# Chain states on ScalarE, attention outputs beside chain outputs, a gate product in rounded parts, and narrower reads in a hybrid attention/RWKV layer

## The chip, the cores and the metric

The kernel runs on one core of a Trainium2 chip. The metric is the device time of one execution in microseconds; the median of several runs is compared. PE is TensorE's matmul, PEld its weight load, DVE is VectorE, ACT ScalarE, POOL GpSimd, SP the engine that issues most DMAs.

## The reference

One layer over 16 meta tokens and 512 tokens of width 1024. A projection of 5632 columns feeds windowed attention with sinks, an RWKV-7 recurrence and two gates; both results are gated, added, projected and normalized; a squared-ReLU MLP of width 4096 and a last normalization follow. The first 16 rows are dropped.

```python
proj = h @ w_in[l]
q, k, v, zr, gate_att, gate_rwkv = jnp.split(proj, [c0, c1, c2, c3, c4], axis=-1)
att = lax.map(lambda qkv: swa_one(qkv[0], qkv[1], qkv[2], rel_bias, sinks_l), (q, k, v))
rw = rwkv7_time_mix(zr, ...)
merged = jax.nn.sigmoid(gate_att) * att + jax.nn.sigmoid(gate_rwkv) * rw
h = layer_norm(ALPHA * h + merged @ w_out[l], ...)
ff = jnp.square(jax.nn.relu(h @ w_ff1[l])) @ w_ff2[l]
h = layer_norm(ALPHA * h + ff, ...)
...
# in rwkv7_time_mix, with z shifted by one token: z + (prev - z) * mu
g = jax.nn.sigmoid(gl) @ g2
def step(S, inp):
    r_t, w_t, k_t, v_t, kk_t, a_t = inp
    sa = jnp.einsum('bhij,bhj->bhi', S, -kk_t)
    S = S * w_t[:, :, None, :] + sa[..., None] * (kk_t * a_t)[:, :, None, :] + v_t[..., None] * k_t[:, :, None, :]
    return S, jnp.einsum('bhij,bhj->bhi', S, r_t)
```

The outputs y of the meta tokens are not used by anything; their effect on the state S is.

## The kernel before

**Large products.** Every weight is split into a rounded part and its rest, both of a type that TensorE multiplies at its fast rate: ScalarE casts (`split`, line 256), VectorE subtracts (line 259). A product is then three matmuls per block of 128 rows: high by high, high by low, low by high (`three`, lines 340 to 342). A *dense unit* makes 128 columns of the input projection: 8 blocks of 3 matmuls, over all 528 tokens in two halves of 264 columns (`ALLT`, and `RSP` for the r units), or over the 512 tokens in one piece (`XT_`). A unit is a generator: one step is one block, three matmuls, and it tells the planner its length, 3 * (0.014 + n / 2400), line 371. When a span is done ScalarE and VectorE take it out of PSUM and mix in the token before (`shifted`, lines 415 to 426).

**Stages.** The 16 heads are worked off in 8 pairs. In stage s the dense units of several pairs run: the gates of pair s-1, k, r and v of pair s+1, and the query of pair s. Between their steps stand the small matmuls of three pairs: the inner scores and block inverse of pair s (`scan`), the solution of pair s-1 (`solve`), and the attention of pairs s-1 and s-2 (`attend`, `attend_out`, `join`).

**The order on PE is written by hand.** Each item has a time; `weave` sorts them and puts an item between the dense steps as soon as the sum of the steps' lengths reaches its time. PE keeps to this order strictly: an item that isn't ready holds up everything behind it. On the other engines a list scheduler sets the order at build time, by priority (`ahead` raises it: 600 for the chain, 400 for evictions, 200 for folds) and by the times that it assumes; at run time each engine's queue is worked in that order.

**The chain.** The recurrence runs over 8 blocks of 64 tokens. `rwkv_fold` (two halves, lines 876 and 881) adds the parts of the transition matrices, on VectorE, into `AX`. `rwkv_chain(j, c)` is one matmul (line 936) from state `Z[c]` into the PSUM bank `ch`; `follow` scales the result into `Z[c + 1]`, one head by VectorE (line 892), the other by ScalarE (line 894). So a link is matmul, two scalings, next matmul. `rwkv_start` uses `follow` too. `rwkv_outputs` (line 953) reads all states; `rwkv_norm` turns the result and line 977 writes it into `z`, of which there is one buffer.

**Attention.** `attention_scores` (two halves) puts products into two PSUM banks of the pool `pat`, which has two; VectorE masks and adds the bias (1108, 1109). After the second half VectorE takes the maxima, and ScalarE makes eight exponentials (1130) and eight scalings (1136). One stage later `attention_turn` transposes the probabilities, ScalarE and VectorE take them out (1151, 1152), and `attention_out` multiplies them with the values into a bank of `pat`, held from its first half to the end of its second; VectorE then multiplies with the gate in place, in `ga` (1172). `merge` adds this to `z` and stores it.

**The rest that is touched.** `gate_rank` makes `sg`, the sigmoid of the gate's low rank, once; `gate_out` multiplies it per pair with `gw`, in full fp32 (line 1088). `rwkv_bonus` makes a sum over a head with two matmuls of 512 columns (595, 596) in a bank of the pool `pg`, which the folds use too. `first_up` loads the first MLP weights into buffers that are free by then.

Of the kernel before, what the change touches and what calls it, by code (L numbers as in the profile page):

```python
# [11 lines left out]
F32 = mybir.dt.float32  # L12
F32R = mybir.dt.float32r
I32 = mybir.dt.int32
AF = mybir.ActivationFunctionType
ALU = mybir.AluOpType
# [4 lines left out]
P = 128  # L21
D = 1024
KT = D // P
SEQ = 512
# [6 lines left out]
NCH = SEQ // C  # L31
PAIRS = HEADS // 2
# [41 lines left out]

CONSTS = {}
PRI = {'load': 100, 'dense': 400, 'scores': 300, 'chain': 600, 'turn': 200, 'up': 300, 'fold': 200, 'start': 200}
RSP = ((0, 264), (264, 264))
HOLD = 4
SBB = 2
WB = (3, 3, 2)  # L80
# [1 line left out]
PS = (2, 2, 1, 1, 2)  # L82
AHEAD = 2
NBUF = {'AX': 2, 'BK': 1, 'NT': 2, 'GR': 2}
ABUF = {'q': 2, 'ga': 1, 'gg': 1, 'pa': 1, 'z': 1, 'bv': 1}


def _constants():
# [42 lines left out]
def hybrid_layer_kernel(ctx: ExitStack, tc: tile.TileContext, I: dict, out: bass.AP):  # L131
    nc = tc.nc
    dve, act, pool, pe = nc.vector, nc.scalar, nc.gpsimd, nc.tensor
# [4 lines left out]
    pg = pps.enter_context(tc.tile_pool(name="pg", bufs=PS[1], space=PSUM))  # L138
    ppr = ctx.enter_context(ExitStack())
    pch = ppr.enter_context(tc.tile_pool(name="pch", bufs=1, space=PSUM, side="right"))  # L140
    pat = ppr.enter_context(tc.tile_pool(name="pat", bufs=PS[4], space=PSUM, side="right"))
# [22 lines left out]
    lz = ctx.enter_context(tc.tile_pool(name="lz", bufs=1))  # L164
# [174 lines left out]
    def three(ps, whi, wlo, xhi, xlo, first=True, last=True):  # L339
        pe.matmul(ps, whi, xhi, start=first, stop=False)  # L340
        pe.matmul(ps, whi, xlo, start=False, stop=False)  # L341
        pe.matmul(ps, wlo, xhi, start=False, stop=last)  # L342
# [61 lines left out]
    at = p2.enter_context(tc.tile_pool(name="at", bufs=1))  # L404
    pew = ctx.enter_context(ExitStack())
    ew = pew.enter_context(tc.tile_pool(name="ew", bufs=1))
# [22 lines left out]


    zz = lz.tile([P, T], F32, name="zz", tag="zz")
    sg = lz.tile([P, SEQ], F32, name="sg", tag="sg")

    rest = CONST.shape[1]
    nc.sync.dma_start(con[:, w0:rest], I["consts"][:, w0:rest])
# [10 lines left out]
        act.copy(zz[HD:P], zl[HD:P])  # L446

    def gate_rank(zg):
        act.activation(sg, zg[:, NMETA:], AF.Tanh, scale=0.5)
        dve.tensor_scalar(sg, sg, 0.5, 0.5, op0=ALU.mult, op1=ALU.add)  # L450

    def B64(ap, n):
        return ap.unsqueeze(len(ap.shape)).to_broadcast(list(ap.shape) + [n])
# [2 lines left out]
    ER = [slice(0, 64), slice(64, 128)]  # L456
# [133 lines left out]
    def rwkv_bonus(j):  # L590
        S = SS[j]
        rkh, rkl = S["rk"]
        S["bv"] = dr.tile([P, SEQ], F32, name=f"bv{j}")
        bp = pg.tile([P, 512], F32, name="bp", tag="g")
        pe.matmul(bp, bones, rkh, start=True, stop=False)
        pe.matmul(bp, bones, rkl, start=False, stop=True)
        bv = ew.tile([P, SEQ], F32, name="bv", tag="rk")
        dve.tensor_tensor(bv, bp, S["v"][:, NMETA:], op=ALU.mult)
        nc.sync.dma_start(S["bv"], bv)
# [286 lines left out]
    def follow(S, c, src, last):  # L886

        Z, PC = S["Z"], S["PC"]
        for e in range(2):
            dst, scale = Z[c][ER[e], e, :], PC[ER[e], last : last + 1]  # L890
            if e == 0:
                dve.tensor_scalar(dst, src[e][ER[e]], scale, None, op0=ALU.mult)  # L892
            else:
                act.activation(dst, src[e][ER[e]], AF.Copy, scale=scale)  # L894

    def rwkv_start(j, n):

# [97 lines left out]
    A = {}  # L995
# [76 lines left out]

    def aside_gate_rwkv(j):

        gw = at.tile([P, P], F32, name="gw", tag="gw", bufs=2)
        nc.sync.dma_start(gw, I["gate_w2"][j])

        def evict(ps, t0, n):
            t = gate_tile("gg", "r", j)
            act.activation(t, ps, AF.Tanh, scale=0.5)  # L1080
            A["gg", j] = t

        A["gw", j] = gw
        yield from dense(COL_GRW + j * P, XT_, evict)

    def gate_out(j):
        gp = pat.tile([P, 512], F32, name="gp", tag="a")
        pe.matmul(gp, A["gw", j], sg, start=True, stop=True)
        t = A["gg", j]
        dve.scalar_tensor_tensor(t, t, 1.0, gp, op0=ALU.add, op1=ALU.mult)  # L1090

# [151 lines left out]
    for n, pools in enumerate((((dn, "dn"), (pat, "a")), ((pg, "g"), (pch, None)))):  # L1243
        for b in range(4):
            pool_, tag = pools[b // 2]
# [20 lines left out]
    def first_up():  # L1266

        A["w1"] = load_pieces("w_ff1", 0, [
            [lz.tile([P, SEQ], F32R, name="w1", tag=t, bufs=ABUF.get(t, 1)) for t in tags]
            for tags in (("zz", "sg"), ("kk", "q"))  # L1270
        ])

    def out_unit(n, blocks, asks):
# [62 lines left out]
    j = PAIRS - 1  # L1336
# [18 lines left out]
    F = partial  # L1355

    def scan(j):

        need = (f"k{j}", f"r{j}", f"v{j}")
        return [  # L1360
            (0.0, need, F(rwkv_scores, j, 0)),
            (3.2, (), F(rwkv_meta, j)),
            (3.2, (), F(rwkv_scores, j, 1)),
            (3.2, (), F(rwkv_inverse, j)),
            (5.6, (), F(rwkv_bonus, j)),
            (12.55, (), F(rwkv_turn_scores, j)),
            (18.6, (), F(rwkv_turn_keys, j)),
            (16.0, (), F(rwkv_inverse_place, j)),
            (23.2, (), F(rwkv_turn_values, j)),
        ]  # L1370

    def solve(j):

        last = j == PAIRS - 1
        return [
            (0.0, (), F(rwkv_blocks, j, 0)),
            (0.0, (), F(rwkv_start, j, 0)),
            (1.4, (), F(rwkv_blocks, j, 1)),
            (1.4, (), F(rwkv_start, j, 1)),
            (3.2, (), F(rwkv_blocks, j, 2)),  # L1380
            (3.2, (), F(rwkv_start, j, 2)),
            (4.6, (), F(rwkv_blocks, j, 3)),
            (6.4, (), F(rwkv_turn_inverse, j)),
            (8.4, (), F(rwkv_fold, j, 0)),
            (10.6, (), F(rwkv_fold, j, 1)),
        ] + [(10.4 + 1.25 * c, (), F(rwkv_chain, j, c)) for c in range(NCH - 1)] + [
            (18.61 + 0.6 * last, (), F(rwkv_outputs, j)),
            (24.6 - 1.4 * last, (), F(rwkv_norm, j)),
        ]
# [11 lines left out]
    def attend(j, t0, dt=3.6):  # L1401
        return [
            (t0, (f"q{j}",), F(attention_scores, j, 0)), (t0 + dt, (), F(attention_scores, j, 1)),
        ]

    def attend_out(j, t0, t1, t2, t3):
        return [
            (t0, (), F(attention_turn, j, 0)),
            (t1, (), F(attention_out, j, 0)),
            (t2, (), F(attention_turn, j, 1)),  # L1410
            (t3, (f"ga{j}",), F(attention_out, j, 1)),
        ]

    def join(j, t0, t1, t2):
        return [
            (t0, (f"gr{j}",), F(gate_out, j)), (t1, (), F(merge_rwkv, j)), (t2, (), F(merge, j)),
        ]

    with tc.manual_schedule(engines={mybir.EngineType.PE}):
        for s in range(-1, PAIRS + 1):  # L1420
            if s <= PAIRS:
                units[:] = [u for u in all_units[: marks[s + 1]] if u[0] not in finished]
            items = []
            if s > 0:
                items += solve(s - 1)
            if 0 <= s < PAIRS:
                items += scan(s)
            if s == -1:
                items += [
                    (0.0, (), F(rwkv_begin, 0)),  # L1430
                    (9.0, ("wa",), F(rwkv_lora, 0, 0)),
                    (10.4, (), F(rwkv_lora, 0, 1)),
                    (20.0, ("k0",), F(rwkv_sums, 0)),
                    (24.0, ("k0",), F(rwkv_begin, 1)),
                ]
            if 0 <= s < PAIRS - 1:
                items += project_in(s + 1)
            if s == 0:
                items += [(18.0, ("av",), F(aside_heads, 0))]
            if s == 4:  # L1440
                items += [(26.0, (), F(aside_heads, 1))]
            if s in (1, 5):
                items += [(2.4, (), turn_heads)]
            if 0 < s < PAIRS - 1:
                items += attend(s - 1, 4.6, 1.8) + join(s - 1, 13.5, 25.4, 0)[:2]
            if 1 < s < PAIRS:

                items += attend_out(s - 2, 7.6, 8.4, 9.4, 10.6) + join(s - 2, 0, 0, 11.6)[2:]
            if s == PAIRS - 1:
                items += [(14.0, (), merged_before)]  # L1450
                items += attend(s - 1, 4.6, 1.8) + attend_out(s - 1, 15.6, 16.6, 16.6, 18.0)
                items += join(s - 1, 15.0, 26.5, 26.5)
                items += attend(s, 11.6, 2.2)
                items += [(27.2, (), F(load_out, q, 0)) for q in range(3)]
            if s == PAIRS:
                items += attend_out(s - 1, 3.0, 5.4, 5.4, 7.8) + join(s - 1, 0.0, 24.5, 25.5)
                items += [(2.0, (), F(merged, s - 2)), (25.6, (), F(merged, s - 1))]
                items += [(3.0, (), residual_gain), (17.0, (), first_up)]
                items += [(3.0 + 3 * b, (), F(residual_rows, b)) for b in range(4)]
            weave(items, True)  # L1460
# [141 lines left out]
    with tc.manual_schedule(engines={mybir.EngineType.PE}):  # L1602
# [26 lines left out]
        pa = ctx.enter_context(tc.tile_pool(name="pa", bufs=1, space=PSUM))  # L1629
# [92 lines left out]
```

## Time and profile before

| | |
|---|---|
| median of 3 runs | 967.89 us (966.96 to 968.17) |
| profiled execution | 965.14 us |
| its span, first to last instruction | 963.3 us |
| granted TensorE clock | 0.998 |
| a steady stage (s = 2, 3, 5) | some 61 us |
| DMA | 99.93 MB, mean 104 GB/s |

The profile comes from one execution. The page lists busy time by engine, then groups of instructions: source line, engine, operation, the tiles written and read, shapes, count, busy time and mean, and the idle time of the engine just before them with what ended it. The waits list who waited for whom: total us, times, longest. The timeline has start and duration of each instruction; PE's durations include the drain of its pipeline, so the distance from start to start is the matmul's price. In fp32 each matmul shows as two instructions. The windows give busy time (and count) of PE, PEld, DVE, ACT, POOL in a stretch, then the granted clock, the DMA share and GB/s.

### The profile page before, as it was taken

Reading aid. Unit: us, or ns where it says so; the run is one execution under the profiler, and the core shown is the slowest. Engines: PE = TensorE matmul, PEld = TensorE weight load, DVE = VectorE, ACT = ScalarE, POOL = GpSimd, SP = SyncE. Lnnn points to the kernel's source line nnn. Section 1 sums busy time; section 2 is a strip of 40 time slices with the busy share of each in tenths; the row PEclk is TensorE's granted clock in tenths of the full one; section 3 lists DMA queues with packets and bytes.
Section 4 is the critical chain, followed back from the end, with each engine's and each line's share of the span. In section 5 each row is a group of like instructions: output and inputs, shape, how many; then the busy total and the mean of one; then the engine's idle time right before and its main releaser. Section 6 shows DMA issues by size and latency. Waiting matters only on the chain.

```text
span 963.3 us, 19229 instructions
## 1 busy us (share of the span) xinstructions
PE 931.8 (97%) x7693; PEld 776.7 (81%) x7693; DVE 631.0 (66%) x1444; ACT 449.9 (47%) x1111; POOL 43.7 (5%) x106
## 2 busy tenths in 40 slices
PE   4999999999999999999999999999999999999996
PEld 3888789798897977978877787988888888888885
DVE  7576888787887879878785958575423244442427
ACT  6535665565565655557447436534312124432120
POOL 2000000010000100000001001000000000000001
PEclk9999999999999999999999999999999999999999
DMA  7544332233333323333333635133232232232222
GB/s 273 95 127 116 85 86 81 76 78 91 88 87 90 84 80 87 78 98 88 112 100 78 242 125 192 59 128 111 88 106 90 92 106 88 90 106 88 86 90 87
DMA packets 79649, 99.93 MB, mean 104 GB/s; under 512 B 47174, under 2 KB 54072, under 8 KB 79560
## 3 DMA queue, kind: packets, MB, share of 16 engines
q1 hardware_dynamic: 78064, 96.63, 33.8%
q10 hardware_dynamic: 1496, 2.08, 0.6%
q8 instruction: 60, 0.98, 0.4%
q14 instruction: 29, 0.24, 0.1%
HBM read 85.23 MB, written 13.47 MB: 102 GB/s over the span
## 4 chain that ended last, share of the span: by engine, by line
PE 78%; DVE 13%; ACT 4%; DMA 2%; issue 2%; POOL 1%; SPq 0%; DVEq 0%; ACTq 0%; POOLq 0%
PE dps L340 14%; PE dps L341 13%; PE dps L342 13%; PE acc L1492 6%; PE acc L1493 6%; PE acc L1494 6%; DVE wlo L259 2%; DVE ftmp L761 2%; PE sp L1102 2%; DVE Xf L765 2%; PE sc L658 2%; DVE AX L881 2%; PE wp L859 1%; PE o L1262 1%; PE o L1263 1%
## 5 line engine op out<-in xcount | busy, mean ns | idle before, releaser
L259 DVE TENSOR_TENSOR wlo<-wraw,whi 128x512 fp32r<-128x512 f32 x240 | 157.6, 685 | 171.5 <-ACT whi L256 170.3
L256 ACT CAST whi<-wraw 128x512 fp32r<-128x512 f32 x240 | 140.6, 617 | 265.3 <-PE dps L341 128.6
L340 PE MATMUL dps<-hhi,whi 128*128 128x264 f32 (+1 forms) x640 | 219.6, 343 | 2.4 <-DVE k L415 1.4
L341 PE MATMUL dps<-hlo,whi 128*128 128x264 f32 (+1 forms) x640 | 203.2, 318 | 1.4 <-DVE hlo L321 1.4
L342 PE MATMUL dps<-hhi,wlo 128*128 128x264 f32 (+1 forms) x640 | 203.4, 318 | 0.2 <-DVE wlo L259 0.2
L340 PEld LDWEIGHTS dps<-hhi,whi 128*128 128x128 f32 x640 | 120.5, 188 | 22.3 <-issue 11.6
L341 PEld LDWEIGHTS dps<-hlo,whi 128*128 128x128 f32 x640 | 120.8, 189 | 8.9 <-DVE hlo L321 2.2
L342 PEld LDWEIGHTS dps<-hhi,wlo 128*128 128x128 f32 x640 | 120.3, 188 | 8.9 <-DVE wlo L259 0.4
L341 PE MATMUL dps<-h1lo,whi 128*128 128x512 f32 (+1 forms) x256 | 97.3, 380 | 0.0
L340 PE MATMUL dps<-h1hi,whi 128*128 128x512 f32 (+1 forms) x256 | 97.3, 380 | 0.0
L342 PE MATMUL dps<-h1hi,wlo 128*128 128x512 f32 (+1 forms) x256 | 97.3, 380 | 0.0
L340 PEld LDWEIGHTS dps<-h1hi,whi 128*128 128x128 f32 x256 | 48.0, 187 | 10.3
L342 PEld LDWEIGHTS dps<-h1hi,wlo 128*128 128x128 f32 x256 | 48.0, 188 | 10.2
L341 PEld LDWEIGHTS dps<-h1lo,whi 128*128 128x128 f32 x256 | 48.0, 188 | 10.2
L1492 PE MATMUL acc<-whi,hhi 128*128 128x512 f32 x128 | 50.6, 395 | 0.0
L1493 PE MATMUL acc<-wlo,hhi 128*128 128x512 f32 x128 | 50.4, 394 | 0.0
L1494 PE MATMUL acc<-whi,hlo 128*128 128x512 f32 x128 | 50.2, 392 | 0.0
L1493 PE MATMUL acc<-wlo,fhi 128*128 128x512 f32 x112 | 43.6, 389 | 0.0
L1492 PE MATMUL acc<-whi,fhi 128*128 128x512 f32 x112 | 43.6, 389 | 0.0
L1494 PE MATMUL acc<-whi,flo 128*128 128x512 f32 x112 | 43.6, 389 | 0.0
L1592 DVE TENSOR_TENSOR rl<-rl 128x512 f32<-128x512 f32 (+1 forms) x36 | 22.8, 632 | 15.1 <-ACT hhi L1591 9.1
L894 ACT ACTIVATE Z<-ch,PC 64x64 f32<-64x64 f32 x56 | 17.3, 310 | 30.9 <-DVE Z L892 30.2
(277 smaller groups left out, 1658.9 us busy)
## 6 DMA issues: line engine op xcount, KB each, us to landing
wraw<-in_w_ff_dram SPq DMA_DIRECT2D x64, 512.0 KB, 3.5
wraw<-in_w_in_dram SPq DMA_DIRECT2D x52, 512.0 KB, 3.5
wraw<-in_w_out_dram SPq DMA_DIRECT2D x8, 512.0 KB, 4.2
xt<-in_x_dram SPq DMA_DIRECT2D x4, 512.0 KB, 6.1
Nd<-NT SPq DMA_DIRECT2D x16, 128.0 KB, 3.1
bv<-bv SPq DMA_DIRECT2D x8, 256.0 KB, 4.5
bvm<-bv SPq DMA_DIRECT2D x8, 256.0 KB, 5.0
XB<-xtd SPq DMA_DIRECT2D x16, 128.0 KB, 3.2
```

The source lines that it names most:

```text
L256: act.copy(hi[:n, qs], raw[:n, qs])
L259: dve.tensor_tensor(lo[:n, qs], raw[:n, qs], hi[:n, qs].bitcast(F32), op=ALU.subtract)
L340: pe.matmul(ps, whi, xhi, start=first, stop=False)
L341: pe.matmul(ps, whi, xlo, start=False, stop=False)
L342: pe.matmul(ps, wlo, xhi, start=False, stop=last)
L658: pe.matmul(scs[d][to, c * P : (c + 1) * P], BK[ER[e], 4 * i + c, to], AXg[ER[e], e, 4 * i + c], start=True, stop=True,)
L761: dve.tensor_tensor(tv, Xf[:, 0:nj, s : s + 1].to_broadcast([NB, nj, nt]), Nf[:, s : s + 1, s + 1 :].to_broadcast([NB, nj, nt]), op=ALU.mult,)
L765: dve.tensor_tensor(Xf[:, 0:nj, s + 1 :], Xf[:, 0:nj, s + 1 :], tv, op=ALU.add)
L1492: pe.matmul(acc[b], xhi[k][:, bs], hi[:, ws], start=first, stop=False)
L1493: pe.matmul(acc[b], xhi[k][:, bs], lo[:, ws], start=False, stop=False)
L1494: pe.matmul(acc[b], xlo[k][:, bs], hi[:, ws], start=False, stop=last)
L1592: dve.tensor_tensor(r, r, r, op=ALU.mult)
```

## The change

Six things. `follow` puts both scalings on ScalarE. The chain's links start at 9.8 and stand 1.4 apart, before at 10.4 and 1.25. In stages 1 to 6 the second half of the scores, the turns, the attention outputs, the merge and the gate product have other times, and `ga` gets a second buffer; in stage 7 their times stay. `rwkv_bonus` uses a bank of `pat` and stands at 7.0, before 5.6. The gate product is made of three rounded matmuls, for which `sg` is rounded once and `gw` per pair. The r units leave out the first 14 tokens: their halves have 258 and 256 columns. `first_up` uses the buffers of the rounded `sg`.

```diff
-RSP = ((0, 264), (264, 264))
+RSP = ((14, 258), (272, 256))
...
-ABUF = {'q': 2, 'ga': 1, 'gg': 1, 'pa': 1, 'z': 1, 'bv': 1}
+ABUF = {'q': 2, 'ga': 2, 'gg': 1, 'pa': 1, 'z': 1, 'bv': 1}
...
-    sg = lz.tile([P, SEQ], F32, name="sg", tag="sg")
+    sghi = lz.tile([P, SEQ], F32R, name="sghi", tag="sghi")
+    sglo = lz.tile([P, SEQ], F32R, name="sglo", tag="sglo")
...
     def gate_rank(zg):
+        sg = ew.tile([P, SEQ], F32, name="sg", tag="v")
         act.activation(sg, zg[:, NMETA:], AF.Tanh, scale=0.5)
         dve.tensor_scalar(sg, sg, 0.5, 0.5, op0=ALU.mult, op1=ALU.add)
+        act.copy(sghi, sg)
+        dve.tensor_tensor(sglo, sg, sghi.bitcast(F32), op=ALU.subtract)
...
-        bp = pg.tile([P, 512], F32, name="bp", tag="g")
+        bp = pat.tile([P, 512], F32, name="bp", tag="a")
...
         for e in range(2):
-            dst, scale = Z[c][ER[e], e, :], PC[ER[e], last : last + 1]
-            if e == 0:
-                dve.tensor_scalar(dst, src[e][ER[e]], scale, None, op0=ALU.mult)
-            else:
-                act.activation(dst, src[e][ER[e]], AF.Copy, scale=scale)
+            act.activation(
+                Z[c][ER[e], e, :], src[e][ER[e]], AF.Copy, scale=PC[ER[e], last : last + 1]
+            )
...
-        gw = at.tile([P, P], F32, name="gw", tag="gw", bufs=2)
+        gw = at.tile([P, P], F32, name="gw", tag="gw")
+        gwh = at.tile([P, P], F32R, name="gwh", tag="gwh")
+        gwl = at.tile([P, P], F32R, name="gwl", tag="gwl")
         nc.sync.dma_start(gw, I["gate_w2"][j])
+        act.copy(gwh, gw)
+        dve.tensor_tensor(gwl, gw, gwh.bitcast(F32), op=ALU.subtract)
...
-        pe.matmul(gp, A["gw", j], sg, start=True, stop=True)
+        three(gp, *A["gw", j], sghi, sglo)
...
-            for tags in (("zz", "sg"), ("kk", "q"))
+            for tags in (("zz", "sghi"), ("kk", "sglo"))
...
-            (5.6, (), F(rwkv_bonus, j)),
+            (7.0, (), F(rwkv_bonus, j)),
...
-        ] + [(10.4 + 1.25 * c, (), F(rwkv_chain, j, c)) for c in range(NCH - 1)] + [
+        ] + [(9.8 + 1.4 * c, (), F(rwkv_chain, j, c)) for c in range(NCH - 1)] + [
...
             if 0 < s < PAIRS - 1:
-                items += attend(s - 1, 4.6, 1.8) + join(s - 1, 13.5, 25.4, 0)[:2]
-            if 1 < s < PAIRS:
+                items += attend(s - 1, 4.6, 3.8) + join(s - 1, 12.4, 25.4, 0)[:2]
+            if 1 < s < PAIRS - 1:
+                items += attend_out(s - 2, 9.6, 10.6, 15.0, 18.6) + join(s - 2, 0, 0, 19.8)[2:]
+            if s == PAIRS - 1:
 
                 items += attend_out(s - 2, 7.6, 8.4, 9.4, 10.6) + join(s - 2, 0, 0, 11.6)[2:]
```

More of the change, by code (lines that the diff above doesn't have):

```diff
@@ L1081, in evict @@
             A["gg", j] = t
-        A["gw", j] = gw
+        A["gw", j] = gwh, gwl
         yield from dense(COL_GRW + j * P, XT_, evict)
@@ L1268, in first_up @@
         A["w1"] = load_pieces("w_ff1", 0, [
-            [lz.tile([P, SEQ], F32R, name="w1", tag=t, bufs=ABUF.get(t, 1)) for t in tags]
-            for tags in (("zz", "sg"), ("kk", "q"))
+            [lz.tile([P, SEQ], F32R, name="w1", tag=t) for t in tags]
+            for tags in (("zz", "sghi"), ("kk", "sglo"))
         ])
```

## The prediction

> **What bounds the kernel now.** I read the page's first part, then one steady stage by windows, then the waits, then the timeline of single links of the chain.
>
> ```profile
> span 963.3 us, 19229 instructions
> PE 931.8 (97%) x7693; PEld 776.7 (81%) x7693; DVE 631.0 (66%) x1444; ACT 449.9 (47%) x1111; POOL 43.7 (5%) x106
> ```
>
> TensorE is busy for 97% of the span, so only two things can shorten it: fewer or shorter matmuls, and the stretches in which TensorE's order, which is written out by hand, stands still. Waits of other engines count only where TensorE ends up waiting.
>
> ```profile
> 410.00:425.00 15.00, 15.00 (x323) 11.10 (x321) 8.86 (x21) 9.74 (x29) 0.20 (x1) 1.00 0.29 83
> 425.00:447.00 22.00, 21.73 (x173) 17.92 (x172) 20.93 (x65) 12.57 (x40) 1.22 (x2) 1.00 0.34 88
> 447.00:472.00 25.00, 24.88 (x215) 23.29 (x215) 19.53 (x45) 13.82 (x35) 2.07 (x3) 1.00 0.44 121
> ```
>
> These are stretches of one stage (s = 5): busy time of PE, weight load, VectorE, ScalarE, GpSimd, then the granted clock. In the middle one VectorE works 20.93 of 22 us and ScalarE 12.57. The clock is 1.00, so no term below is one of clock.
>
> ```profile
> ACT Z L894 <- DVE Z L892: 34.0, 36, 3.5
> PEld ch L936 <- ACT Z L894: 6.0, 15, 0.5
> ```
>
> The waits name one recurrent stall of TensorE between the start-up and the output projection: the chain's matmul (line 936) waits for the state Z. Its weight load stood idle 15 times, for 6.0 us. And ScalarE's half of Z waits for VectorE's half, 36 times. One stalled link and one in time, on PE:
>
> ```profile
> 446.06 0.28 PE L342 MATMUL dps<-hhi,wlo 128*128 128x264 f32 x1
> 446.62 0.49 PE L936 MATMUL ch<-Z,AX 128*128 128x128 f32 x2 [0.27 <-ACT Z L894]
> 446.87 0.37 PE L340 MATMUL dps<-hhi,whi 128*128 128x264 f32 x1
> ...
> 448.30 0.28 PE L342 MATMUL dps<-hhi,wlo 128*128 128x264 f32 x1
> 448.42 0.38 PE L936 MATMUL ch<-Z,AX 128*128 128x128 f32 x2
> 448.56 0.37 PE L340 MATMUL dps<-hhi,whi 128*128 128x264 f32 x1
> ```
>
> Starts are what counts, since ends are modelled. From the dense matmul to the one after the link it is 0.26 us in time and 0.81 stalled: the stall costs 0.55 us. What made the first one late, and the shape of a link in time:
>
> ```profile
> 444.56 0.64 DVE L765 TENSOR_TENSOR Xf<-Xf,ftmp 66x28 f32<-66x28 f32 x1
> 445.95 0.27 DVE L892 TENSOR_SCALAR Z<-ch,PC 64x64 f32<-64x64 f32 x1
> 446.26 0.31 ACT L894 ACTIVATE Z<-ch,PC 64x64 f32<-64x64 f32 x1 [0.84 <-DVE Z L892]
> ...
> 448.84 0.28 DVE L892 TENSOR_SCALAR Z<-ch,PC 64x64 f32<-64x64 f32 x1 [0.86 <-PE ch L936]
> 449.15 0.31 ACT L894 ACTIVATE Z<-ch,PC 64x64 f32<-64x64 f32 x1 [0.97 <-DVE Z L892]
> 449.74 0.38 PE L936 MATMUL ch<-Z,AX 128*128 128x128 f32 x2
> 449.81 0.62 ACT L256 CAST whi<-wraw 128x512 fp32r<-128x512 f32 x1 [0.35 <-PE dps L341]
> 450.46 0.48 ACT L421 ACTIVATE k<-dps,drv 128x264 f32<-128x264 f32 x1
> 450.97 0.31 ACT L894 ACTIVATE Z<-ch,PC 64x64 f32<-64x64 f32 x1
> 451.33 0.49 PE L936 MATMUL ch<-Z,AX 128*128 128x128 f32 x2
> ```
>
> The first stall: VectorE reached Z at 445.95 only, behind the block inverse in its queue. The second (link at 451.33): ScalarE had a weight cast and an eviction ahead of Z, because a dense unit ended at the link before. A hop without a queue, from 448.42: VectorE starts after 0.42, ScalarE 0.31 later and takes 0.31, some 0.05 to PE: 1.09 us.
>
> **The change part by part.**
>
> *States by ScalarE, links wider.* VectorE loses 64 operations of 0.27 us (17 us), ScalarE gains 64 of 0.31 (20 us); in the middle stretch it had 9 us free. The hop's bare length hardly moves: 0.42 + 0.31 + 0.31 + 0.05 = 1.09 us, since the halves were serial already. What goes is VectorE's queue, and with the new times the steps between links. A step of a unit of 264 columns is 3 matmuls and moves the planner's clock by 0.372 (line 371). From the listed times the links stood 2, 4, 3, 4, 3, 3 steps apart and will stand 2, 4, 4, 4, 3, 4 apart. The 3-step links at 446.62 and 451.33 are the two stalls; both get a fourth step, 3 x 0.122 = 0.37 us more. The one that stays, 448.42 to 449.74, has 1.32 us for a hop of 1.09. So the first kind of stall goes. In the second the pair takes 0.31 more on ScalarE and has 0.37 more room: 0.1 to 0.3 us may stay per stage. Bounds: 0 (every stall returns elsewhere) and -6.0 (all go). I take -5.0, that is all but some 0.15 in six stages.
>
> *Gate product in rounded parts.*
>
> ```profile
> 444.49 0.28 PE L342 MATMUL dps<-hhi,wlo 128*128 128x264 f32 x1
> 444.61 1.02 PE L1088 MATMUL gp<-sg,gw 128*128 128x512 f32 x2
> 445.06 0.69 PE L340 MATMUL dps<-hhi,whi 128*128 128x264 f32 x1
> 445.58 0.28 PE L341 MATMUL dps<-hlo,whi 128*128 128x264 f32 x1
> ...
> 426.60 0.40 PE L595 MATMUL bp<-rkh,bones 128*128 128x512 f32 x1
> 427.06 0.39 PE L340 MATMUL dps<-hhi,whi 128*128 128x512 f32 x1
> ```
>
> Without the product L341 would have started 0.12 after 444.61, at 444.73; it came at 445.58: 0.85 us. Three rounded matmuls of 512 columns take 0.23 each by the two of line 595 and 596 (0.46 us from 426.60 to 427.06): 0.69. Eight products: 8 x 0.16 = -1.3 us. The Trainium skill's FP8 and Floating Point Precision, TensorE Precision Notes, says a true fp32 product takes four passes; four against three would be 8 x 0.23 = -1.8 us (an estimate); the rows say 0.85 and not 0.92, so the sum keeps -1.3. The rounding itself (per pair a copy and a subtraction of 128x128, once each of 128x512) is work of ScalarE and VectorE long before the product; a 128x512 operation takes 0.64 us on VectorE (line 881 below, 1.27 for two) and 0.62 on ScalarE (line 256 above), which bounds the small ones from above. The dense units, which need nothing of it, cover it; uncovered it would be 1.3 us at the start, once, and at most as much per pair.
>
> *No reads for meta tokens.* Eight units, two halves of 24 matmuls, from 264 columns to 258 and 256.
>
> ```profile
> 447.20 0.29 PE L342 MATMUL dps<-hhi,wlo 128*128 128x264 f32 x1
> ...
> 600.03 0.28 PE L340 MATMUL dps<-h1hi,wk 128*128 128x256 f32 x1
> 602.50 0.28 PE L340 MATMUL dps<-h1hi,whi 128*128 128x256 f32 x1
> ```
>
> Nine matmuls of 264 from 447.20 to 448.30 are 0.122 us apart; 21 of 256 from 600.03 to 602.50 are 0.118. So 24 x (0.003 + 0.004) x 8 = -1.4 us; bounds 0 and, by columns alone (14 of 528 of 48 x 0.122), -1.2 to -1.5. The evictions shrink with it.
>
> *Attention.* The second half of the scores moves from 6.4 to 8.4, the two turns and outputs from 7.6-10.6 to 9.6-18.6, the merge from 11.6 to 19.8, the bonus to another bank. The matmuls are the same in number; two masks, the gated output and the merge, four operations of 0.64, leave VectorE's full stretch or go to its end, and the next one has 5.5 us free. `ga` gets a second buffer because gate and output now live side by side. New tight places: (1) the first link stands at 9.8, with fold 0 at 8.4:
>
> ```profile
> 433.44 1.16 PE L876 MATMUL gq<-GR,WT 64*128 64x128 f32 x16
> 435.20 1.27 DVE L881 TENSOR_TENSOR AX<-AX,gq 128x512 f32<-128x512 f32 x2
> 436.36 0.60 PE L1146 MATMUL pt<-con,sb 128*128 128x128 f32 x4
> 438.19 0.38 PE L936 MATMUL ch<-Z,AX 128*128 128x128 f32 x2
> ```
>
> Today 1.7 us lie between the additions' end (436.47) and the link; afterwards only two steps of 0.69 and a turn of at most 0.60 lie between the fold's end (434.59) and it, so it is due at some 436.5, as the additions end. (2) The bonus (7.0) takes one of the two banks that the scores (8.4) want, 1.4 us later, and VectorE must have read it. (3) The single `z` must be merged and stored before line 977 rewrites it (24.6): 4.8 us of the planner's time instead of 13; what it would hold up first is ScalarE, busy for only 13.82 of 25 us there. Queued behind the late link, score or `z` are the dense matmuls, VectorE's inverse and ScalarE's evictions. Each place costs between 0 and one operation ahead of it, 0.27 to 0.64 by the rows above, per stage; I take 0.7 us in all, nearer to 0, since two of the three have room.
>
> Sum against the execution's own time, 965.14 us (span 963.3 and 1.8 around it): -5.0 - 1.3 - 1.4 + 0.7 = **-7.0 us**, 958.1. The runs' median is 967.89, so the median should become **960.9 us**.
>
> **The rivals.**
>
> *All stalls go, nothing new:* -6.0 - 1.3 - 1.4 = -8.7, 959.2 us. For it: VectorE's full stretch is relieved by more than I count.
>
> *The stalls are replaced:* fold to first link, and the banks, cost 1.0 us in each of six stages: -7.7 + 6.0 = -1.7, 966.2 us, within 0.2% (1.9 us), about what a measurement can tell from no change. For it: the 436.5 above, and in-order queues.
>
> *Narrower matmuls don't pay:* if the spacing is set by the weight load, the 1.4 us stay: 962.3 us. Against it: 0.118 at 256 columns. The Trainium skill's TensorE: Matmul & The Clock Gate, Back-to-back issue gap, has the spacing set by both the matmul and its weight load; by that rule a floor is possible, and the trace so far shows none down to 256.
>
> *Slower: the softmax stands in front of the links on ScalarE.*
>
> ```profile
> 434.49 0.39 ACT L1130 ACTIVATE sb<-sb,nm 128x128 f32<-128x128 f32 x1
> ...
> 437.19 0.39 ACT L1130 ACTIVATE sb<-sb,nm 128x128 f32<-128x128 f32 x1
> ...
> 440.09 0.31 ACT L894 ACTIVATE Z<-ch,PC 64x64 f32<-64x64 f32 x1
> 440.43 1.87 ACT L1136 ACTIVATE sb<-sb,sm 128x128 f32<-128x128 f32 x6
> ```
>
> Eight exponentials are 0.39 apart (3.1 us), eight scalings 0.31 (2.5 us). They start 2 us later than now, over links 0 to 3. A link four steps apart has 1.69 - 1.09 = 0.6 us to spare. If one pair stands behind all exponentials and one behind all scalings: 2.5 + 1.9 = 4.4 us a stage, 26 in six: -7.0 + 26 = +19, 987 us. It decides from (7.0 + 1.9) / 6 = 1.5 us a stage, five operations ahead of one link. Against it: at 440.09 a Z stands between scalings, ahead of the other six.
>
> **How the numbers follow.** Forecast 960.9 (own range 959 to 963): 0.55. All gone 0.13, floor 0.05, replaced 0.15, slower 0.12. Faster by over 0.2%: 0.55 + 0.13 + 0.05 = 0.73; within: 0.15; slower: 0.12. The range leaves out the last and reaches below 959.2 by a microsecond and over 966.2 by one: 958 to 967.
>
> **What would show it.** Right: no wait of ScalarE's Z for VectorE; weight-load idle before line 936 under 1.5 us instead of 6.0; three matmuls per gate product, 0.69 us from start to start; 0.118 us at 256 columns. Wrong: a wait of line 936 for the additions of line 881, of the scores for a bank, or of Z behind line 1130 or 1136; then the stalls sit there. If the clock is below 1.00 the sum doesn't hold.

## The result, and the profile after

The changed kernel takes 974.73 us (median of 5 runs, 974.51 to 978.02), the kernel before 967.81 us beside it: a ratio of 1.0086 with a 95% interval of 1.0067 to 1.0105 (the ratio is estimated from all runs of both, so it isn't exactly the quotient of the medians). It is slower, by 7 to 8 us; 960.9 was forecast. The profiled execution took 974.73 us.

The page of the changed kernel begins (busy us, share of the span, instructions):

```profile
span 972.9 us, 19278 instructions
...
PE 929.4 (96%) x7701; PEld 777.6 (80%) x7701; DVE 620.9 (64%) x1389; ACT 471.2 (48%) x1184; POOL 44.6 (5%) x106
```

The span grew by 9.6 us, and TensorE's busy time fell by 2.4. So the matmuls did become cheaper, and TensorE stands still for 12 us more. The last two stretches of the same stage as in the prediction, shifted by the 8.85 us by which it starts later (busy us of PE, weight load, VectorE, ScalarE, GpSimd, then the clock):

```profile
433.85:455.85 22.00, 21.15 (x165) 18.15 (x164) 18.94 (x61) 11.99 (x39) 1.56 (x3) 1.00 0.30 80
455.85:480.85 25.00, 23.68 (x213) 21.81 (x212) 18.46 (x41) 16.20 (x42) 1.76 (x2) 1.00 0.39 109
```

TensorE now idles 0.85 us in the first of them and 1.32 in the last, where it idled 0.27 and 0.12. VectorE's full stretch did become emptier (18.94 for 20.93), as intended; that alone did not help. What TensorE waits for, by the waits of the changed kernel (total us, times, longest):

```profile
PEld ch L938 <- ACT Z L894: 8.0, 13, 1.1
PEld ss L568 <- ACT sq L517: 4.6, 6, 0.8
PE ch L938 <- DVE Xf L769: 4.7, 5, 1.3
PE ch L938 <- DVE AX L885: 0.8, 1, 0.8
```

(Line 936 is 938 now, 894 stayed, 881 is 885, 765 is 769, 1130 and 1136 are 1136 and 1142.) There are three waits instead of one kind: a link for ScalarE's state, the sums of squares for their squares, and a link for VectorE. PE's timeline in the steady stage of the windows shows each:

```profile
444.01 0.60 PE L1152 MATMUL pt<-con,sb 128*128 128x128 f32 x4
445.46 0.46 PE L938 MATMUL ch<-Z,AX 128*128 128x128 f32 x2 [0.85 <-DVE Xf L769]
...
456.44 0.38 PE L938 MATMUL ch<-Z,AX 128*128 128x128 f32 x2
...
457.63 0.28 PE L342 MATMUL dps<-hhi,wlo 128*128 128x264 f32 x1
458.73 0.49 PE L938 MATMUL ch<-Z,AX 128*128 128x128 f32 x2 [0.81 <-ACT Z L894]
...
461.08 1.04 PE L719 MATMUL tr<-con,BK 128*128 128x128 f32 x8
462.63 1.09 PE L568 MATMUL ss<-con,sq 128*64 128x2 f32 x16 [0.51 <-ACT sq L517]
```

**The first link** was due about 0.44 us after the turn at 444.01 (so far apart the two stand where nothing is waited for, in the fourth experiment) and came at 445.46: 1.0 us lost. Its releaser is named as the inverse, but the link reads only `Z` and `AX`; the name is that of the VectorE operation that ended last (at 445.44), and the addition in front of it is the one it needs. VectorE's timeline:

```profile
442.17 0.42 DVE L1114 COPY_PREDICATED sp<-con,sp 128x256 f32<-128x256 int32 x1
...
442.64 0.41 DVE L1115 TENSOR_TENSOR sb<-sp,bias 128x256 f32<-128x256 f32 x1
...
443.11 0.42 DVE L1114 COPY_PREDICATED sp<-con,sp 128x256 f32<-128x256 int32 x1
...
443.57 0.41 DVE L1115 TENSOR_TENSOR sb<-sp,bias 128x256 f32<-128x256 f32 x1
...
444.04 1.27 DVE L885 TENSOR_TENSOR AX<-AX,gq 128x512 f32<-128x512 f32 x2
```

The fold's matmuls had been done by 442.6. Four operations of the second half of the scores, with steps of the inverse between them, stand ahead of the additions, which end at 445.31.

**The late link** was due at 457.75 (0.12 after the last dense matmul) and came at 458.73: again 1.0 us. ScalarE's timeline:

```profile
455.61 0.62 ACT L894 ACTIVATE Z<-ch,PC 64x64 f32<-64x64 f32 x2
456.25 0.69 ACT L1142 ACTIVATE sb<-sb,sm 128x128 f32<-128x128 f32 x2
456.98 0.59 ACT L1157 COPY pall<-pt 128x512 f32<-128x512 f32 x1
457.46 0.69 ACT L1142 ACTIVATE sb<-sb,sm 128x128 f32<-128x128 f32 x2
458.05 0.62 ACT L894 ACTIVATE Z<-ch,PC 64x64 f32<-64x64 f32 x2
...
461.19 0.63 ACT L894 ACTIVATE Z<-ch,PC 64x64 f32<-64x64 f32 x2
461.84 0.74 ACT L517 ACTIVATE sq<-k,vc 128x528 f32<-128x528 f32 x1
```

The link before it stood at 456.44, so its states could have begun 0.42 later, at 456.86. They began at 458.05: four scalings of the softmax and the copy of the turned probabilities are worked first. **The sums:** the squares stand behind the last pair of states, end at 462.58, and TensorE lost 0.5 us.

One measure is used below beside the ratio. The first `up` matmul of a solution marks a stage's start; the *step* is the mean of three steady stages (s = 2, 3, 4), and *seven stages* is the distance from the first such mark to the eighth. In the changed kernel such marks stand at 230.63 and 293.43 us, for instance, which makes a step of 62.80; before it is 61.29 there. By this count the stage of the windows is s = 6, not 5 as the prediction has it; its argument doesn't depend on that. Stage 5, which the table of the time before counts among the steady ones of some 61 us, takes 62.5 by it. All runs, in us:

| kernel | step | seven stages | median | ratio to before, interval |
|---|---|---|---|---|
| before | 61.31 | 427.29 | 967.81 | |
| after | 62.76 | 436.30 | 974.73 | 1.0086, 1.0067 to 1.0105 |
| a_old_attn | 60.85 | 425.05 | 963.10 | 0.9974, 0.9959 to 0.9990 |
| a_link0_late | 61.96 | 431.18 | 971.20 | 1.0055, 1.0035 to 1.0074 |
| a_follow_dve | 62.42 | 435.99 | 973.58 | 1.0080, 1.0065 to 1.0095 |
| b_gate_r | 61.53 | 428.11 | 966.14 | 1.0000, 0.9988 to 1.0013 |
| a_scores_early | 61.36 | 426.91 | 966.38 | 0.9993, 0.9977 to 1.0008 |
| b_attn | 63.63 | 440.99 | 981.02 | 1.0142, 1.0121 to 1.0163 |
| a_old_attn_dve | 60.90 | 426.00 | 963.35 | 0.9962, 0.9945 to 0.9978 |
| a_old_attn_sums | 60.48 | 422.81 | 960.99 | 0.9937, 0.9922 to 0.9951 |
| a_sums | 62.35 | 433.71 | 973.56 | 1.0073, 1.0057 to 1.0089 |
| a_early_sums | 60.90 | 424.58 | 963.05 | 0.9967, 0.9955 to 0.9979 |
| b_links_bank_sums | 60.86 | 425.01 | 963.40 | 0.9966, 0.9952 to 0.9979 |
| b_links_bank | 61.09 | 426.28 | 964.31 | 0.9982, 0.9972 to 0.9992 |

(The seven stages of a_follow_dve hold a stretch at half the clock, worth up to 1.7 us; see the end.) The loss lies in the first of the seven stages (+2.6) and in the five steady ones (some +1.4 each); the seventh, where the attention kept its times, is 0.8 shorter.

### The profile page after: what moved, and what is told of

Read it like the earlier page. It is cut to its first block, busy times and chain, and to the rows that moved or that the text cites. A ratio compares the mean times of both kernels' runs of the same rounds, so it can differ in the third digit from the quotient of the medians.

```text
span 972.9 us, 19278 instructions
## 1 busy us (share of the span) xinstructions
PE 929.4 (96%) x7701; PEld 777.6 (80%) x7701; DVE 620.9 (64%) x1389; ACT 471.2 (48%) x1184; POOL 44.6 (5%) x106
## 4 chain that ended last, share of the span: by engine, by line
PE 75%; DVE 11%; ACT 10%; issue 2%; DMA 2%; POOL 0%; SPq 0%; DVEq 0%; ACTq 0%; POOLq 0%
PE dps L340 14%; PE dps L341 12%; PE dps L342 12%; PE acc L1500 6%; PE acc L1501 6%; PE acc L1502 6%; ACT sb L1142 2%; ACT Z L894 2%; PE sc L662 2%; PE wp L863 1%; DVE ftmp L765 1%; DVE wlo L259 1%; PE o L1268 1%; DVE Xf L769 1%; ACT whi L256 1%
## 5 line engine op out<-in xcount | busy, mean ns | idle before, releaser
L340 PE MATMUL dps<-hhi,whi 128*128 128x264 f32 (+3 forms) x640 | 217.1, 339 | 3.0 <-DVE k L415 1.7
L341 PE MATMUL dps<-hlo,whi 128*128 128x264 f32 (+3 forms) x640 | 202.9, 317 | 1.3 <-DVE hlo L321 1.3
L342 PE MATMUL dps<-hhi,wlo 128*128 128x264 f32 (+3 forms) x640 | 203.0, 317 | 0.2 <-DVE wlo L259 0.2
L894 ACT ACTIVATE Z<-ch,PC 64x64 f32<-64x64 f32 x112 | 34.5, 308 | 28.4 <-PE ch L938 27.4
L938 PE MATMUL ch<-Z,AX 128*128 128x128 f32 x112 | 23.7, 293 | 10.8 <-ACT Z L894 5.3
```

What stands on the lines that cost most here:

```text
L894: act.activation(Z[c][ER[e], e, :], src[e][ER[e]], AF.Copy, scale=PC[ER[e], last : last + 1])
L938: pe.matmul(ps, GQ[:, c, 0].rearrange("p e t -> p (e t)"), Z[c].rearrange("p e i -> p (e i)"), start=True, stop=True,)
```

## The experiments

The theory: the attention's new times are the cause. They put VectorE's and ScalarE's work for the scores ahead of the fold's additions and of the states. The rivals: ScalarE is overloaded by its second scaling; or the first link simply stands too early.

**The attention's times of before, in the changed kernel** (a_old_attn).

```diff
-                items += attend(s - 1, 4.6, 3.8) + join(s - 1, 12.4, 25.4, 0)[:2]
-            if 1 < s < PAIRS - 1:
-                items += attend_out(s - 2, 9.6, 10.6, 15.0, 18.6) + join(s - 2, 0, 0, 19.8)[2:]
-            if s == PAIRS - 1:
+                items += attend(s - 1, 4.6, 1.8) + join(s - 1, 13.5, 25.4, 0)[:2]
+            if 1 < s < PAIRS:
```

> The changed kernel with the attention, merge and gate-product times of before; the rest of the change stays. Theory 1 (the moved attention makes the two large stalls of a stage: the scores put VectorE work between the fold and its additions, and softmax and turn stand on ScalarE ahead of a state): both go, some 2 us in each of six stages, span about 961. Theory 2 (both scalings on ScalarE make them, whatever stands beside): the late link still waits 0.9 us or more and the span stays above 968.

Ratio 0.9974, the step 1.91 us shorter than in the changed kernel. The waits:

```profile
PEld ss L568 <- ACT sq L517: 3.7, 6, 0.7
...
PEld ch L938 <- ACT Z L894: 0.9, 2, 0.7
```

In the steady stages no link waits at all. The wait for the squares stays, so it has another cause.

**The first link later** (a_link0_late): the time of link 0 is 10.6, as it nearly was (10.4).

```diff
-        ] + [(9.8 + 1.4 * c, (), F(rwkv_chain, j, c)) for c in range(NCH - 1)] + [
+        ] + [(10.6 if c == 0 else 9.8 + 1.4 * c, (), F(rwkv_chain, j, c)) for c in range(NCH - 1)] + [
```

> The changed kernel with the first link at 10.6 instead of 9.8, behind the second fold; all other links stay. Theory 1 (the first link stands too close behind the first fold): its wait of 1.0 us in six stages goes, span about 967. Rival (the wait is only handed to the next link, which now has 1.4 us instead of 3.7): span 971 or more, and the second link's matmul waits.

Ratio 1.0055. The first link's wait is gone, and most of it comes back at another link, the fourth and not the second that the rival named. The span, 968.1, lies between the two forecasts. By the waits:

```profile
PEld ch L938 <- ACT Z L894: 12.2, 16, 1.0
```

The link that had waited 0.14 us, about 34 us into the stage, now waits 0.92, since TensorE reaches it a microsecond earlier and ScalarE doesn't; the late one waits 0.79 instead of 0.98. The gain that remains, 0.8 us a stage, comes with the wait for the squares, which goes. So the early link alone is not the cause.

**VectorE's half of the state back** (a_follow_dve): `follow` as before, all else as in the change.

```diff
-            act.activation(
-                Z[c][ER[e], e, :], src[e][ER[e]], AF.Copy, scale=PC[ER[e], last : last + 1]
-            )
+            dst, scale = Z[c][ER[e], e, :], PC[ER[e], last : last + 1]
+            if e == 0:
+                dve.tensor_scalar(dst, src[e][ER[e]], scale, None, op0=ALU.mult)
+            else:
+                act.activation(dst, src[e][ER[e]], AF.Copy, scale=scale)
```

> The changed kernel with the scalings as before, one head on VectorE, one on ScalarE. Theory 2 (the second scaling in ScalarE's queue makes the late link and the sums of squares late): these two waits, about 1.5 us in each of six stages, go: span about 964, the first link still waits 1.0 us. Theory 1 (they come from the moved softmax and turn): the late link still waits about as long, span 970 to 975.

Ratio 1.0080: no gain that the intervals can tell; the step is 0.34 shorter. In a steady stage the first link still loses 1.01 us, later ones 0.51, 0.14 and 0.82. As the cause of the links' waits, the rival of ScalarE's second scaling falls. It does explain the wait for the squares, which shrinks from 4.6 us of the weight load's idle time to 1.0; by the waits of this kernel:

```profile
PEld ss L568 <- issue: 1.0, 6, 0.2
```

**One number: the second half of the scores back at 6.4** (a_scores_early).

```diff
-                items += attend(s - 1, 4.6, 3.8) + join(s - 1, 12.4, 25.4, 0)[:2]
+                items += attend(s - 1, 4.6, 1.8) + join(s - 1, 12.4, 25.4, 0)[:2]
```

> The changed kernel with only the second half of the scores back at 6.4 (8.4 in the change); turns, outputs and merge stay late. If the scores between fold and additions make the first link wait, and the softmax that they set off makes the late link wait: both waits fall from 1.0 to under 0.3 us in six stages, span about 962. If the late turn (15.0) with its copy on ScalarE makes the late link wait: that one stays near 1.0, span about 967. If neither, 972.

Ratio 0.9993; the step is 1.40 us shorter. PE's and VectorE's timelines of this kernel at the first link:

```profile
438.12 0.60 PE L1152 MATMUL pt<-con,sb 128*128 128x128 f32 x4
438.56 0.39 PE L938 MATMUL ch<-Z,AX 128*128 128x128 f32 x2
```

```profile
437.03 1.27 DVE L885 TENSOR_TENSOR AX<-AX,gq 128x512 f32<-128x512 f32 x2
```

The masks are out of the way, the additions end at 438.30, and the link comes 0.44 after the turn. The late link's wait goes too: maxima, exponentials and scalings all hang on the second half, and start 5 to 6 us earlier in the stage. So a single number of the change made both 1.0 us waits. (The span, 964.9, is above the expected 962; one stretch at half the clock, at the start, is in it.) What is left over against a_old_attn (0.5 us a stage) is the first attention output, which stands close behind its turn; by the waits of this kernel:

```profile
PEld ss L568 <- ACT sq L517: 3.9, 6, 0.7
...
PEld av L1172 <- DVE pown L1158: 2.9, 5, 0.8
```

**The attention's times alone, in the kernel before** (b_attn, with `ga` in two buffers).

```diff
-ABUF = {'q': 2, 'ga': 1, 'gg': 1, 'pa': 1, 'z': 1, 'bv': 1}
+ABUF = {'q': 2, 'ga': 2, 'gg': 1, 'pa': 1, 'z': 1, 'bv': 1}
...
-                items += attend(s - 1, 4.6, 1.8) + join(s - 1, 13.5, 25.4, 0)[:2]
-            if 1 < s < PAIRS:
+                items += attend(s - 1, 4.6, 3.8) + join(s - 1, 12.4, 25.4, 0)[:2]
+            if 1 < s < PAIRS - 1:
+                items += attend_out(s - 2, 9.6, 10.6, 15.0, 18.6) + join(s - 2, 0, 0, 19.8)[2:]
+            if s == PAIRS - 1:
```

> The kernel before with only the attention, merge and gate-product times of the change and the second gate buffer; links at 10.4 + 1.25 c, scalings on both engines. If the moved attention alone makes the loss: span 968 or more, the late link waits 0.8 us or more in stages 2 to 6; the first link, 0.6 later than in the change, waits less than 0.5. If it takes the early first link as well: span 962 to 966.

Ratio 1.0142, 14 us slower: more than the whole change. PE's timeline has the worst link, ScalarE's what stood in front of it:

```profile
457.61 0.38 PE L936 MATMUL ch<-Z,AX 128*128 128x128 f32 x2
460.64 0.49 PE L936 MATMUL ch<-Z,AX 128*128 128x128 f32 x2 [1.55 <-ACT Z L894]
```

```profile
458.28 0.39 ACT L1130 ACTIVATE sb<-sb,nm 128x128 f32<-128x128 f32 x1
...
458.79 1.07 ACT L698 COPY AT<-axt 128x512 f32<-128x512 f32 x2
459.75 0.41 ACT L1130 ACTIVATE sb<-sb,nm 128x128 f32<-128x128 f32 x1
...
460.27 0.31 ACT L894 ACTIVATE Z<-ch,PC 64x64 f32<-64x64 f32 x1
```

VectorE's half began at 458.03, 0.42 after the link. ScalarE's half comes at 460.27, behind exponentials and the copies that the scan needs: 1.75 us lost in one link of each stage, 2.9 in all its links. With the other parts of the change beside it the loss is smaller, by 4.7 us over the seven stages (440.99 to 436.30).

**The gate product and the narrower r alone, in the kernel before** (b_gate_r).

```diff
-RSP = ((0, 264), (264, 264))
+RSP = ((14, 258), (272, 256))
...
-        pe.matmul(gp, A["gw", j], sg, start=True, stop=True)
+        three(gp, *A["gw", j], sghi, sglo)
```

(with the rounding of both factors as in the change)

> The kernel before with only the gate product in rounded parts and the narrower r units. By the sum of the prediction -1.3 and -1.4 us: span 960.6, 965.1 us against 967.8. Rival (the rounding or the weight load gives it back): span 963 or more.

Ratio 1.0000. The matmuls are shorter here too, but PE's timeline shows who gets the time:

```profile
449.69 0.28 PE L342 MATMUL dps<-hhi,wlo 128*128 128x264 f32 x1
450.39 0.49 PE L940 MATMUL ch<-Z,AX 128*128 128x128 f32 x2 [0.42 <-ACT Z L898]
```

The product stands between two links. TensorE reaches the second one earlier and waits for its state: 0.58 us, before 0.43. The last link still waits 0.30, before 0.29:

```profile
454.94 0.28 PE L342 MATMUL dps<-hhi,wlo 128*128 128x258 f32 x1
455.36 0.49 PE L940 MATMUL ch<-Z,AX 128*128 128x128 f32 x2
```

And a link between these two, in time before, now waits 0.13. ScalarE's timeline shows what is new in front of its state:

```profile
450.37 0.30 ACT L1083 CAST gwh<-gw 128x128 fp32r<-128x128 f32 x1
450.69 0.48 ACT L421 ACTIVATE k<-dps,drv 128x264 f32<-128x264 f32 x1
```

The rounding of `gw` stands ahead of an eviction. VectorE's part of that eviction begins at 451.25 and its half of the state at 451.66, 1.27 us behind the link at 450.39; in the kernel before it was 0.95 behind. So the links wait some 1.0 us a stage, before 0.72, and the dense matmul behind a link that waited starts 0.24 us after it, not 0.14. Together that is some 0.4 us a stage, more than the 0.3 that the shorter matmuls save (0.15 at the product, 0.14 in the r unit), and the rival of the rounding is right for a part of it. The step is 0.2 us longer; the last 0.1 of that is a gap between two dense matmuls 58.4 us into the stage, which was not followed.

**VectorE's half of the state, with the attention of before** (a_old_attn_dve: a_old_attn with `follow` as before).

> The changed kernel with the attention times of before and the scalings of before: what is left is wider links, gate product, narrower r, bonus. If the wider links alone end the stalls of before: no link of stages 2 to 6 waits over 0.1 us, and the sums of squares (late by 0.5 us a stage behind the pair of scalings on ScalarE) wait no more: steps of some 60.2 us a stage, span 958. If the scalings on ScalarE were needed for it: the 0.3 to 0.4 us stalls of before are back, steps of 61.0 or more.

Ratio 0.9962 against 0.9974, the step 60.90 against 60.85: no difference. The links then wait 0.32 and 0.13 us a stage, so the stalls are partly back, but the squares no longer come late. What ScalarE's states win at the links they lose at the squares; the step lies between the two forecasts, 60.2 and 61.0.

**The sums of squares later** (a_old_attn_sums: a_old_attn with one more number).

```diff
-            (25.5 if j == 1 else 18.6, (f"k{j}",), F(rwkv_sums, j)),
+            (25.5 if j == 1 else 20.0, (f"k{j}",), F(rwkv_sums, j)),
```

> The changed kernel with the attention times of before and the sums of squares at 20.0 instead of 18.6. They wait 0.5 us for ScalarE's square in each of six stages when they stand at 18.6; 1.4 later that should be gone: steps of 60.3 us a stage instead of 60.8, span 958 to 959, faster than both kernels. If the wait moves to what stands behind them: 60.8.

960.99 us, ratio 0.9937, 0.9922 to 0.9951: faster than both kernels. The windows of its steady stage that answer to those above:

```profile
422.70:444.70 22.00, 22.00 (x180) 18.65 (x180) 20.73 (x64) 14.42 (x46) 1.57 (x2) 1.00 0.29 84
444.70:469.70 25.00, 25.00 (x274) 23.30 (x273) 18.79 (x43) 14.86 (x37) 2.46 (x3) 1.00 0.48 128
```

TensorE has no idle time, with VectorE as full as before (20.73 of 22). VectorE's load was not the limit there; the order was.

**The sums later in the changed kernel** (a_sums: that number alone).

> The changed kernel with one time altered: the sums of squares (tile ss) stand at 20.0 instead of 18.6. In the changed kernel TensorE waits there 0.5 to 0.8 us in each of six stages for ScalarE's squares (line 517), which stand behind the last pair of states. Theory: that wait comes from the last link, which now stands at 18.2 (9.8 + 6 x 1.4) instead of 17.9, and from both of its scalings on ScalarE; it has nothing to do with the attention and its price adds to that of the two late links. Then the wait goes and nothing else moves: 974.7 - 6 x 0.6 = 971.1 us, ratio to the kernel before 1.0045 to 1.006, waits of the links unchanged at about 1.0 + 1.0 us a stage. Rival: the 0.6 us turn up at the next thing that needs ScalarE or VectorE there (turn of the keys, the v unit's bank), since the chain's end sets the pace: 974 us, ratio 1.008.

Ratio 1.0073, the step 0.41 shorter, the waits of the links unchanged. The median (973.56) lies nearer to the rival, the step at two thirds of the theory's 0.6. The wait is a cause of its own, and a smaller one than the theory had it.

**Two numbers** (a_early_sums: scores at 6.4 and sums at 20.0 in the changed kernel).

> The changed kernel with the second half of the scores back at 6.4 and the sums at 20.0: two single numbers altered, the outputs, merge, gate product and second buffer as in the change. Theory (the parts add): the first brought 974.7 to 966.4, the second takes another 3.5: 962.5 to 963.5 us, ratio 0.995 to 0.9965; what is left over against the kernel with the attention of before and the sums at 20.0 (960.99) is the wait of the attention output for the turned probabilities, about 0.3 us a stage. Rival (the late links take over): with the sums later the last links stand free but the turn and its copies still meet a late link, ratio 0.998 or more.

963.05 us, as the theory has it; the ratio, 0.9967, is 0.0002 above its range. The parts add (the step falls by 1.40, then by 0.46), and two numbers of the order are worth 1.2% of the kernel's time, the difference between 1.0086 and 0.9967.

**The best kernel without gate product and narrower r** (b_links_bank_sums).

> The kernel before with ScalarE's states, the wider links, the bonus in the other bank and the sums at 20.0, that is the best kernel so far (960.99) without the gate product in rounded parts and without the narrower r units. Added to the kernel before alone, those two brought 0.0 us (ratio 1.0000), though the matmuls took 2.2 us less. Theory: they brought nothing there because a link that waits for its state uses up what was saved in front of it; where no link waits they pay in full: this kernel then takes 961.0 + 2.2 = 963.2 us, ratio 0.9955 to 0.9968. Rival: the saved matmul time is swallowed in any case (by the r and v units' ends, which wait for banks), and this kernel takes the same 961.0 us, ratio 0.9935 to 0.9945.

963.40 us, ratio 0.9966, as the theory has it; the step 60.86 against 60.48: the two parts that brought nothing to the kernel before bring 0.38 us a stage here, where no link waits.

**States, wider links and the bonus's bank alone** (b_links_bank).

```diff
-        bp = pg.tile([P, 512], F32, name="bp", tag="g")
+        bp = pat.tile([P, 512], F32, name="bp", tag="a")
...
-            (5.6, (), F(rwkv_bonus, j)),
+            (7.0, (), F(rwkv_bonus, j)),
...
-        ] + [(10.4 + 1.25 * c, (), F(rwkv_chain, j, c)) for c in range(NCH - 1)] + [
+        ] + [(9.8 + 1.4 * c, (), F(rwkv_chain, j, c)) for c in range(NCH - 1)] + [
```

(and `follow` as in the change)

> The kernel before with ScalarE's states, the wider links and the bonus in the other bank, and nothing else: the part that the prediction priced at -5.0 us, alone. Theory: the stalls of the links (0.72 us a stage) go, but two more places where a link stands alone between dense matmuls take some 0.1 us each, and the sums of squares at 18.6 now wait 0.4 us for ScalarE; the sum is -0.72 + 0.2 + 0.4 = -0.1 us a stage, -0.6 us in all: ratio 0.998 to 1.0005, steps between stages 61.2 us. Rival (the prediction's step): the stalls go and nothing comes for them: -5.0 us, ratio 0.9945 to 0.9955, steps 60.5 us.

Ratio 0.9982, in the theory's range; the step 61.09, 0.1 below it. The links' stalls of a steady stage fall from 0.72 to 0.08 us. The wait for the squares appears:

```profile
PEld ss L564 <- ACT sq L513: 4.0, 6, 0.7
```

One detail of the expectation was wrong: in the stage that was counted, TensorE leaves the dense matmuls 20 times, as in the kernel before. It is 22 times with the sums at 20.0, so the later sums bring the two interruptions, not the links.

## Why the prediction was wrong, by its steps

**The bound** was read rightly: the order on PE and what it waits for set the time, not the load of an engine.

**The failed step is that on the attention**: "Each place costs between 0 and one operation ahead of it, 0.27 to 0.64", and "I take 0.7 us in all". From a_old_attn to the changed kernel the seven stages grow by 436.30 - 425.05 = 11.3 us. The mechanism of place (1) was seen, with the right instant ("as the additions end"), but priced by one operation; the traces show four masks and biases of 0.41 to 0.42 us ahead of the additions, all released by the very instruction that the change moved beside the fold. The step counted what the moved scores cost on TensorE (nothing) and what leaves VectorE's full stretch. It counted them as two masks and did not put the four operations of lines 1108 and 1109, which move with their matmul, into VectorE's queue at their new time. Places (2) and (3), the bonus's bank and the single `z`, add no wait of their own to TensorE's lists: near 0, as taken. Not among the three places was the output close behind its turn, the 0.5 us a stage of a_scores_early.

**The rival "slower"** had the mechanism for the other half: softmax ahead of a state on ScalarE. It was held unlikely because a `Z` stood between scalings in the trace of before. b_attn shows it beyond its deciding point of 1.5 us a stage (2.9 us of link stalls, 2.2 more than before), with both the exponentials and the scan's copies in front. With the change's wider links it is 1.0 us a stage, and together with the first link's 1.0, which the rival "replaced" had, it passes that point. The two were priced as alternatives, and both came. The rival's "They start 2 us later than now, over links 0 to 3" was off as well. The planner's time counts the dense steps alone; on the chip the second half of the scores starts 16.6 us into the stage before and 20.5 after, the first exponential 23.3 and 28.4, the last scaling 30.7 and 38.6. So the softmax moves by 5 to 8 us and stands beside links 1 to 5; link 5, the last that it meets, is the late one.

**Links and states, -5.0:** the stalls did go, and ScalarE no longer waits for VectorE's half. The term was mis-sized: alone the part gives -1.0 us over the seven stages (426.28 against 427.29) and a ratio of 0.9982, some -1.7. The bare links win 0.64 us a steady stage. The squares, which stand behind the last pair of states on ScalarE, take back 0.2 to 0.4 (0.23 by the step of b_links_bank_sums, 0.42 by what TensorE waits there), a place that the prediction did not name although it said that each pair takes 0.31 more there. And the first of the seven stages is 0.9 longer in this kernel than before (60.65 for 59.79); its links lose only 0.3 more, and the rest was not followed.

**Gate product -1.3 and narrower r -1.4:** right at the instruction, not in what it brought. PE's timeline of the changed kernel:

```profile
450.45 0.39 PE L340 MATMUL gp<-sghi,gwh 128*128 128x512 f32 x1
450.68 0.39 PE L341 MATMUL gp<-sglo,gwh 128*128 128x512 f32 x1
450.91 0.40 PE L342 MATMUL gp<-sghi,gwl 128*128 128x512 f32 x1
451.15 0.28 PE L340 MATMUL dps<-hhi,whi 128*128 128x264 f32 x1
```

0.70 us from start to start, forecast 0.69, before 0.85. In the r unit:

```profile
459.18 0.28 PE L341 MATMUL dps<-hlo,whi 128*128 128x258 f32 x1
...
460.38 0.28 PE L342 MATMUL dps<-hhi,wlo 128*128 128x258 f32 x1
```

Ten matmuls in 1.20 us: 0.120 each at 258 columns, no floor down to there. As a sum, -2.7 was forecast. The two parts together measure +0.8 us over the seven stages in the kernel before, -1.2 with the links mended (the second gate buffer with them), -2.2 with the squares mended too. What the prediction lacked is the condition: time saved on TensorE in front of a wait is given to the wait. And "the dense units ... cover it" did not hold for the rounding: in b_gate_r the cast of `gw` makes one more link late, by 0.13 us a stage.

Put together over the seven stages: -1.0 (links) - 1.2 (matmuls) + 11.3 (attention), some +9.0, which is 436.30 - 427.29. The three are differences along one path of kernels (before, b_links_bank, a_old_attn, changed), so that they add up is no proof; on another path the parts have other sizes, as b_attn's +13.7 for the attention alone shows.

## What to carry to other kernels

When an instruction is moved in a hand-made order, move what it releases on the other engines too, and write their queues at the new time, the chip's and not the planner's: the price is the whole train of operations that it lets loose ahead of a critical one, not one operation. Price a saving on the bounding engine only up to the next wait behind it; remove the waits first, then the work. Before calling such a change bad, undo its numbers one by one: one number here made two waits in two engines' queues.

## What the runs showed of the hardware that was not expected

TensorE's clock was at half for one stretch of 3.4 us in six of the fourteen profiled executions (apart from the last microseconds of each): at 26.6 to 26.9 us in three, and at 90.8, 512.8 and 540.7 us. The windows of a_old_attn have one in the output projection, with the stretch before it:

```profile
537.30:540.70 3.40, 2.32 (x44) 1.76 (x43) 3.34 (x7) 1.50 (x4) 0.00 (x0) 1.00 0.87 309
540.70:544.10 3.40, 3.40 (x39) 2.31 (x37) 3.40 (x6) 1.15 (x4) 0.00 (x0) 0.50 0.62 233
```

By the granted clock of 0.50, 3.4 us do the work of 1.7, so the execution is up to 1.7 us longer (an estimate), as much as some of the parts measured here. That is why the steps, which such a stretch outside them can't touch, stand beside the ratios. The Trainium skill, TensorE: Matmul & The Clock Gate, Part 1, has the clock fall after an idle window of about 3.4 us. Here it fell after a stretch in which TensorE was busy for 2.32 of 3.40 us, and for 1.6 to 2.0 us ahead of the other five. Yet five waits of 1.6 us, one in each steady stage of b_attn, brought none, though TensorE was busy for only 1.8 to 1.9 of the 3.4 us around each. So idle time goes ahead of all six stretches and doesn't suffice; what decides stays open.
